# Two decoder layers on one core: q and k by features instead of by transposed tokens

## The chip, the cores and the metric

One core of a Trainium2 chip. The metric is the device time of one launch in microseconds. All arithmetic of the reference is in float32, and the kernel keeps nearly that precision in its big products by splitting each operand.

## The reference, cut

Two layers on 256 tokens of width 1024, with 8 heads of 128. Since the 256 keys are one block, layer 0's block-sparse attention is plain causal attention with a bias; layer 1 takes the difference of two softmax maps per head. Each layer ends in a SwiGLU of width 2816.

```python
for i in range(2):
    sh_a, sc_a, g_a, sh_f, sc_f, g_f = split(silu(c) @ ada_w[i] + ada_b[i])
    h = rms_norm(x, g0) * (1 + sc_a) + sh_a
    q, k, v = split(h @ w_qkv[i])                       # 256 x 1024 each
    # layer 0: p = softmax(q k' / sqrt(128) + bias), causal; o = p v
    # layer 1: heads in two halves of 64: a = softmax_1 - lam * softmax_2; o = rms_norm(a v)
    x = x + g_a * rms_norm(o @ w_o[i], g1)
    h = rms_norm(x, g2) * (1 + sc_f) + sh_f
    x = x + g_f * rms_norm((silu(h @ Wg) * (h @ Wu)) @ W_out, g3)
```

## The kernel before

**Tiles.** The 256 tokens are two tiles t = 0, 1 of 128. An activation that enters a big product lies transposed: `h[t]` is 128 features x (2, 8, 128): hi and lo part, 8 blocks k of features, 128 tokens. `h[t]` for t = 0 and t = 1 are buffers of two classes, `h0` and `h1`, one each.

**Products.** A float32 operand is split in hi (rounded to the fast type float32r) and lo (the rest). `mm` (line 488) makes a product of 128 tokens by up to 512 features for one block k in three passes q: hi x hi, hi x lo of the weights, lo of h x hi. For each pass and each output tile it issues one matrix instruction (line 492): the stationary operand is `h[t]` of that block, 128x128, and 512 columns of weights stream. In the profile each such instruction is a weight load (PEld) and a product (PE). Weights come by DMA into `raw` buffers (line 482), ScalarE writes the hi part (483), VectorE the lo part (484) into a ring of nine `s_...` tiles.

**q and k.** The scores need q and k with features on the partitions. `qk_T` (line 576) does it: ScalarE copies 128 tokens x 512 features out of PSUM (583; q is scaled there), PE transposes the four heads (`transposes`, 296), and ScalarE copies them into `qT` or `kT` (585), 128 features x 4 heads x 256 tokens. A group g is four heads.

**Order in layer 0.** `first_block` (675) makes q and k of group 0 and q of group 1 while the first modulation vectors are still loading: it goes through k in steps of 1, 2, 2, 2, 1 blocks, and for each step loads modulation weights, modulates both tiles' h (`modulate`, 500: ScalarE 508 and 513, VectorE 514) and adds the products of these blocks to six PSUM tiles. Then `build_bias` (316) makes the table of the relative bias in DRAM, from which `load_bias` reads it back by head; k of group 1, the scores and softmax of group 0 (`softmax`, 587: scores 603, bias 606, exp 611), v and the softmax of group 1 follow; `attend` (640) multiplies with v, and then come the output product, the norm and the feed-forward.

**Order in layer 1.** For each group and tile, q and k together (`mm` with two output tiles), then `qk_T` for both; v last.

**What sets the order of all work.** The functions only describe operations with engine, an assumed cost, and what they read and write. A planner (`Schedule`) issues them in the order that a table `PRIORITIES` of one number per operation and these costs lead to, under limits on buffers: PSUM tiles `a` (4) and `bc` (4), the classes `s2`, `raw`, `ring` and others. Each engine then works through its own queue in that order. All loads go through SP's queue.

Of the kernel before, what the change touches and what calls it, by code (L numbers as in the profile page):

```python
# [846 lines left out]
od6sF00000IRFg+0{{vD001xmMF124D*!<NSO9MTh5(!ZvjD^Z&j7mt+W_+c(*f!L^8rEuBLQmxc>#z4y#c)esR73UDFXcgv;md@*#YeV`T;Kjg#sG_Zvv+R  # L847
j{?>J9|AA|n*zZB0|Vv(F9T)+W&>^mQ~|#NCj;^TO#*`gjsvR$$OC%=p#!}G%mXI`mjvSj`2!FH!2^K=j0Cj<Uj%go8~}L$+yO%ZodLN3-U0>#E&>VybOWLT
cLIC@`2!*ZJp^h5R0K!_mIRUnodlc$0R%V%2n22gw*^rIxdr<L%>?iS3I(YJx&)^L;RGlJJ_S_;<OKu<8V0Kd`UDXLf(3#FF$PEmYXx@&eg=sK!UoL-Cj~PF
nFU-1X9jWx<N^r;N(6BPb^|Q~xCGw>zXMVO2L(9=n*-wmVFif=zy-<$)dl1QG6pRMH3lmMz6SdS2L@{gr3Xg_v<K@4fd-WZt_H;hLIzj{at4zI5eHNUYX_wV  # L850
=m!-D`UXA+f(I-Ja0rJ8*aq(gC<p%sSqNnalm?&%<OT`|LkLa?;slfgCI(9ez61vaYzCeNm<5Xk>;^^$xdq+@Z3mhMy9d$--3P`8BnT)7G6>)XMhJfhsRzXf
{0No@9SPwHhzNBEq6oPNu?X}C4hb{~y9m+<=?MP_d<pFdLkVRGlL@H_zzNq076~B<CJHeMbPCQ2EeSXYS_v8oJPJq(mj=8B{RcJ(Q3z`Y-v=oNMG0RCdI^*X
1PTudBnl`BGYSI;X$hzaJqlzBbqY`lp$g9me+rfgtP1c72MZ|++6v_gKnueP#S1(PDG4S3-Uw3)xC-V9c?(Mn=?wD<hYQ#X+Y0{+6by<Cv<v|aN(*ia!3$yw
NerS4ObD_GHwqpLQwv-Rs0*wMx(k&E`w4#v#0wq_cno+9lMI*)3<{A8E)1Rw)C?01Ee)s*v<*cGs|w-@zYWR_)(zne7!D*3ISyP7u@1Wo*bFiZpA6&-6%INM
$qrr)+z#&!X%E8?HxP9X4iJ<P%Mn%!kqgrc>I)VO7YrQ?hztV_PYqfPk`0{=Mh;O9cn*vXq7K*&<PPr+`VIyU5f3I0Uk|hoW)1fZ4-fYb91uYePY_!WsuA81
><!Eg@eWrHJ`Xz(%@A`C&Jykt4hy;r;tYZhnGdiJRSH`S2@S>%-4FB+pbLHtz6}ZxO%Ra~j19&Q0uYf9kr1d5UktDfOb)&f)e!6umI(_Bf(rr>84)27=?hN{
g$+g#T@iE<9S(mF$`6VW%@O1g{}CS&P7L%65e;SzGY_l}MG&bFoDk&@h!8gsZV_M+fDwlgC=*B%77aKJFAjeWtPa8s91rag1QHq&F%n1;ND|}{`w|foJ`+_F
YZHPKnG?nn=o2gyO%%x#Nf4P3;}LffUJ_Ci;1mrNDHcf<ixLYHVikrJo)y3q<`w!CVHSZF?Gf`8$`#QT0T*N#Z4t;49tn{O!wJp`Ee(_oN)0U!)D3VCQxCWh
R}1?P<PS;_P!Vntc?pdXjt;F7_!FTOIu@`IIub7xtQB?;CK4?Wj1q|v&k_g`DHFdCgcFn!78Irtbrf$C>J&;Ae-%|0iWPSjyB7Qv9u{pFB@>ktW)db9$`jrd
ToeHoyA+-lBNgoywG~zuZx+}WN*M<kG#SnqbQt>>e;7X*Um33%UJ{iOWfT7sHWXJBo(d}rD+~$`I1vF7<PS#?^AQRXXA{5^+!AFJu@nLnw-t64+7y`<92aaA  # L860
(iWZ<-4j9-P83-bWE5}|dlZHg>=gGDMirJ7+7;y$2NsPMCKt39$rs=k>=zCg85krOuM@iy0u>Dv85JZIQWaelXccr7xD~?{&lT|%KNd<Ck{6s8ychQuFc>=+
Mi^ZfIv8>oau}Hyrx<1!mKeww>KO1C5g8a6IvGeAX&I#%n;G31))~ba=Nb4J8yY+sJ{m0=0vhZZ0~;k9k`(q7fECdeH5bhn5*C6Mq!zChHy1(|SQlm&ZWntO
hZm?9)fWO7QW$6$tQfZ#!x-5Z<roqf9T_MYnHI(tiWrp`p&0NORT*I!Y#DbMgBgw)nHjqo#u?EW^BMjb2^tj|AQ~$gHyT13J{eaUWEp-Mj2e9zdm618&l=Sl
B^&)3P8(bsmmB39gB!RT9ULwkKO9gTXdH<g3mp0z*c<5^f*hwDQx<a<DHu%}WEy)Kx)z@p3mK6bs2aZ-Oc#n7z!}vV>>2|bc^6t4`574-FdIi3-xqWm@ETnk
bQ_Bs=N6+HN*kdY&Kvt19T;;Ps~Zs<C>%c=Y8gZu9UN60Y#f6eu^bT{&mYep&mWl_nH<L)-5m5B3mqXHI2}(NWgU|psU5%_*B$L01Rfh6UmkTHqaL{)=N|nY
D<4ZAYaiJk{~sS9jT<=~-yM7%F&;=BGaC*bP#%mP&>j>Y?i<n_7#<)Wd>?!tJQ{BurX7MGydMQ1W*DLy<QoMb4Ir5yUmV&V5g(c$o*?ZYgB_tB*dFa5iy@jJ
8y{96n;@DY%OSKP)FKQcfFrph{Ud51(jc87ogo(@7a|uT7a|uTP9jbsP9laPog(-mJR?#gX(KBnD<mr<cqES`>LfZPdL`o}114=I0~!e(Kpn3bJ0grCCmt9h
Pa_f`iX+4$&mTk}{2;_2#31Y;B_qQl+9S#$;UW$r@FNE#7bT`7yd={kh$Xfq%q1=*L?v4#Cmf$0xE?(qQy<PC+#L=fp&^JP79(mTiy_}6up|v8ofc0fIv0y3
!47jKsU|ru+AqB(%PlD`UoL|n03!e+G$czTVk8D0VIg5503~uIpCzOs3MD}$`6Uo0CMItlA|iGoJtkBpY9_WK0VFphm?khNT`1imJ|w0jbSRN1qbMaMjV8z@
xhTvi;wX|Mh9%S`_$VnUKPh1;eJPeI$tv_J#U|V)@+KfBHYa)~kte7pz9-cu>?av0Mkoy_St)BNk13let|`wc_9-ALHY!mn^eRXzIV?FWH7yGvlOo(AMkjG7  # L870
(I`<Ulqt_C=_C^;N++%+2`6MHfhJ8S0w~@o2P$hS)+!n+IV*oEu`0tVS1W5Psw?p-1S?1@yDQf#Dl7*iQYFqKm?eZI04Ja&gC}$(3n&UFO(=6FkSHo90x6j(
EiBnB6)ut}CMtR=j4MDabu5i1yeK~@g)E&cvn-e?#VhzL#w_0~^eogUbSk+j3oRinQZ30R#wiXeXf3QQ!z~pmPAi2g<t-5|5-wOOSS)`mKQ31;Yc3Ti`6)yy
fi9XZuP)IpyDwlcfiO)m$S&P3^)3uABQH@eW-om&lrO<A*)Q!c2rx7-NicOVxG=ad(J<&R{4f<UDltPbSuqqc-!uO+9yI?YxF_!?LoIMG`7cs0moOADP%9TN
*)ZlS6D(FNIW2xIku4oCjWC8WsxMeEZ!w%PJ2Fx-voXps;4x@2e=@8x4l<T98#Rb187jjnyetGO{4B*R2QCRIhAu`d#xBw;7%z<~e=jgFqA*J{VKas^4lgq>
&ox6g_cfh2O*is5i8o6*QaG(Sjyb<NQ8@xT{S`zzN)lo_qZ-#cAv_~JpgkZwcRXc2v_8czBQa_*_c0_g@G=`QK{9eO2QwZsG&6B9kulpbS2JxhgfloWb~39n
u`|ds^)t>c#W15W3p64$IW+Dvoix-m1T{!C=QVCG>@b8e6gDe1LN?_wRyB<^$~N~l+Bf?*YB)<djX91vPc&vUeKeCasx-hf*EH@lGBsZ{b~TJO&^1^#Z#ITD
oHnyI;5H;TJ2z4{Xg7a1oHyAw2RJ%7h&cW%D=tSbtuY=pRW>y>)HVw@i7)IoF*w6A+A^CnqcyrU{xuFa!#7GemN%?7@Hb&NcsQjv9XK>NjyMfDa5-=}zc|l0
<2W-t0zke#r9fjs+C%d~9YothAw@4kg+;GG!bNjK2u4drd`gW^tx#x0GDgKk1xR5=pGX}^1xw{fbxVdy@=GyJ^iWMoPEo&6|50mF|59sHtT0?Re>XrmKsmHI
wKA<W&o#?A);Z!iCNtqQ4K*7&EIKSY9x^;NT{U?-c{_SL7d3P_={bfwojbNWg*A{iu{OCoLOfYK**42K`#4-YX*_d0-8g7Ej5>2Xi9DS=x;)N2<UIR4DLrL5
d^v|Xk~y9^sX4$oIyyx<NIG#kaXOefm^zv|nmXY+DLW}UDLbM&ygL{?XFSI|-#pYk|2-x?m^M~8rZ}fJ&^bRkRxy?`<T6P*@jE{}?K$!}cRIZ~y*fHO{yRoI  # L880
t32C0`#k$R@;G=quREqV$vFo)Dm_#^Ts?<9hdrP@#y#Ra>^%uS7e4Ae2tGJIT0UStfj)>nsXn+q**^C^?LG}ZEI&Oz8$V7zW<QWWfIrYbkw2n8=s!$A*g70L
Z#&~V?>p)|!9C<X_dNwZ7(P2bPd-{cd_IUio<6ERlRmXRz&^}A*FNGt&pxw1^*-7^=sy8J*FP&j2|#5)gFuZytU$X!;Xn*Q^+0ApPeCj}K0#nXctM##l0l<E
#X+<|5JFi(^Eq2QmOP3-pg*}k5jv<l=sV9p=0E*E7dt0Cay=73DnLO%g*p&DIXzcEZa{=U&N_-b@I0G9vOvf{@;enidp_Sl_CO**d_6TlY(P0dP(ge_KR~-d
AVLO19Ydu<-$NHfIz+}p2Sg`CoI$cd$wA;j_CXCoBtkkuQ9@`!enOQ(tU|&<*+TF_G($>5VMBOBjzhvj%|q!!azv~}*F{o9xkT1P!Wk49F&U;A%R~o7UPYrt
c}0jtwnh9!ghazc<U|WaG)2!vzC{5>Kt^9i+(wB;=SF`<qegB<oJI{tPDj{0>poaNDnvp=UPLQADnfTcZAAV=7Da(PpFSTyDn&j;Sw-tWz(VXoW<`WWnMGnh
# [61 lines left out]
```

## Time and profile before

| | |
|---|---|
| time, median of 3 runs | 648.08 us (648.01 to 648.24) |
| the profiled execution, its own time | 645.48 us |
| its span, first to last instruction | 643.7 us |
| PE busy, VectorE busy, ScalarE busy | 627.5, 475.0, 372.5 us |
| loaded from DRAM | 158.69 MB |
| mean granted clock of PE | 0.999 |

A row of PE counts the time in which at least one product's record is open. The records overlap, so the sum of the groups is larger than this time, and the mean of a record is longer than the step from one product to the next.

### The profile page before, as it was taken

The numbers are of one execution on the slowest core, as the hardware profiler recorded it, in microseconds if no ns is written. First come the engines' busy times: TensorE is split into PE (matmuls) and PEld (weight loads), VectorE is DVE, ScalarE is ACT, GpSimd is POOL, SyncE is SP. The second block draws the span as 40 slices with busy tenths as digits, with TensorE's granted clock in tenths as the row PEclk, the third lists the DMA queues.
The fourth block names the chain that finished last, engine by engine and source line by source line (L and its number), as shares of the span: only waits on it lengthen the run. The fifth ranks groups of instructions, "written<-read, shape, count | busy, mean of one in ns | idle before, by whom it ended". The sixth has DMA issues, their size and how long they took to land.

```text
span 643.7 us, 8416 instructions
## 1 busy us (share of the span) xinstructions
PE 627.5 (97%) x2955; PEld 515.0 (80%) x2955; DVE 475.0 (74%) x602; ACT 372.5 (58%) x628; POOL 30.0 (5%) x66
## 2 busy tenths in 40 slices
...
GB/s 291 360 363 319 300 378 381 347 292 249 301 285 353 363 313 270 233 174 293 351 233 194 291 218 271 133 229 72 190 262 163 187 272 224 250 199 180 128 1 66
DMA packets 72487, 160.58 MB, mean 249 GB/s; under 512 B 5491, under 2 KB 22516, under 8 KB 72444
## 3 DMA queue, kind: packets, MB, share of 16 engines
...
q14 instruction: 20, 0.16, 0.1%
q10 hardware_dynamic: 192, 0.08, 0.0%
HBM read 158.69 MB, written 1.33 MB: 249 GB/s over the span
## 4 chain that ended last, share of the span: by engine, by line
PE 85%; DMA 5%; DVE 3%; ACT 3%; POOL 2%; issue 1%; SPq 1%; DVEq 0%; POOLq 0%; ACTq 0%
PE pf L492 19%; PE pg L492 16%; PE pu L492 16%; PE pq L492 10%; PE pv L492 6%; PE po L492 5%; PE pgu L492 3%; DMA bias<-toep 3%; PE ps L603 2%; PE pa L296 1%; PE po L649 1%; PE ph L296 1%; ACT hm L508 1%; DMA toep<-bd 1%; PE pg L419 1%
## 5 line engine op out<-in xcount | busy, mean ns | idle before, releaser
L492 PE MATMUL pg<-s_i,h 128*128 128x512 f32 x480 | 188.3, 392 | 0.0
L492 PE MATMUL pu<-s_i,h 128*128 128x512 f32 x480 | 187.1, 390 | 0.0
L484 DVE TENSOR_TENSOR s_i<-w_i,s_i 128x1024 fp32r<-128x1024 f32 (+1 forms) x96 | 107.0, 1133 | 50.7 <-ACT s_i L483 49.7
L492 PE MATMUL pf<-s_u,a 128*128 128x512 f32 x528 | 137.4, 392 | 0.0
L483 ACT ACTIVATE s_i<-w_i 128x1024 fp32r<-128x1024 f32 (+1 forms) x96 | 93.1, 989 | 73.3 <-PE pu L492 48.8
L492 PEld LDWEIGHTS pf<-s_u,a 128*128 128x128 f32 x528 | 97.9, 188 | 20.4 <-ACT s_u L483 0.4
L492 PEld LDWEIGHTS pg<-s_i,h 128*128 128x128 f32 x480 | 90.1, 188 | 18.8 <-DVE s_i L484 0.3
L492 PEld LDWEIGHTS pu<-s_i,h 128*128 128x128 f32 x480 | 90.1, 188 | 18.4
L362 DVE SCALAR_TENSOR_TENSOR acc<-aw,cact,acc 128x1024 f32<-128x1024 f32 x70 | 89.3, 1277 | 2.2 <-DMA aw<-in_ada_w_dram 1.8
L483 ACT ACTIVATE s_u<-w_u 128x1024 fp32r<-128x1024 f32 x44 | 46.4, 1059 | 58.3 <-PE pu L492 28.8
L484 DVE TENSOR_TENSOR s_u<-w_u,s_u 128x1024 fp32r<-128x1024 f32 x44 | 53.6, 1221 | 30.2 <-ACT s_u L483 29.8
L492 PE MATMUL po<-s_o,o 128*128 128x512 f32 x192 | 49.8, 399 | 0.0
L492 PE MATMUL pq<-s_q,h 128*128 128x512 f32 x192 | 47.7, 397 | 1.8 <-ACT h L513 1.8
L492 PEld LDWEIGHTS pq<-s_q,h 128*128 128x128 f32 x192 | 35.0, 188 | 10.5 <-ACT h L513 2.5
L484 DVE TENSOR_TENSOR s_q<-w_q,s_q 128x1024 fp32r<-128x1024 f32 x32 | 38.5, 1220 | 5.9 <-ACT s_q L483 5.6
L492 PEld LDWEIGHTS po<-s_o,o 128*128 128x128 f32 x192 | 34.9, 188 | 6.8 <-DVE o L665 0.4
L492 PE MATMUL pq<-s_q,hq 128*128 128x512 f32 x144 | 37.0, 408 | 2.5 <-ACT hq L513 2.5
L483 ACT ACTIVATE s_q<-w_q 128x1024 fp32r<-128x1024 f32 x32 | 33.3, 1054 | 4.8 <-PE pq L492 2.0
L492 PEld LDWEIGHTS pq<-s_q,hq 128*128 128x128 f32 x144 | 27.5, 195 | 9.2 <-ACT hq L513 3.0
L471 POOL TENSOR_SCALAR ms<-ss 128x1 f32<-128x1 f32 x16 | 7.3, 459 | 504.7 <-ACT z L542 497.9
L611 ACT ACTIVATE sx<-sx,mx 128x128 f32<-128x128 f32 (+1 forms) x48 | 21.3, 445 | 10.6 <-DVE mx L609 10.6
L492 PE MATMUL pgu<-s_i,h 128*128 128x512 f32 x96 | 26.1, 392 | 0.0
...
## 6 DMA issues: line engine op xcount, KB each, us to landing
...
```

The lines of the kernel that those rows point to most:

```text
L296: nc.tensor.transpose(dst[:, o:o + n], a, ident[:n, :n])
L362: op("DVE", tt(n) + 0.065, lambda: nc.vector.scalar_tensor_tensor(a.t, w(), cact[:, kc:kc + 1], a.t, op0=OP.mult, op1=OP.add), r=[cact, w. ...
L419: nc.tensor.matmul(pg[:, n * j + b:n * j + b + 1], w[:, e, j, b * 128:b * 128 + 128], cact[:, kc + e:kc + e + 1], start=kc + e + j + b == ...
L471: op("POOL", 0.16, lambda: nc.gpsimd.tensor_scalar(ms.t, m0.t[:], 1.0 / n, EPS, op0=OP.mult, op1=OP.add), r=[m0], w=[ms])
L483: op("ACT", ac(2 * n), lambda: nc.scalar.activation(b[:, 0], w.t[:], AF.Copy), r=[w], w=[(b, K(0))], name="hi" + name)
L484: op("DVE", tt(2 * n), lambda: nc.vector.tensor_sub(b[:, 1], w.t[:], b[:, 0].bitcast(F)), r=[w, (b, K(0))], w=[(b, K(1))], name="lo" + name)
L492: nc.tensor.matmul(p[:, :n], a, b[:, 1 if q == 1 else 0, s], start=first and q == 0, stop=last and q == 2)
L508: op("ACT", ac(128, 2, fps), lambda i=i, k=k: nc.scalar.activation(m[:, i], src[2](i), AF.Identity, bias=sh[:, k:k + 1], scale=G[:, k:k + 1]),
L603: nc.tensor.matmul(p[:, i * nk:i * nk + nk], qT[rows, h0 + i, t * 128:t * 128 + 128], kT[rows, h0 + i, 0:nk], start=True, stop=True)
L611: op("ACT", ac(nk, 2), lambda i=i, sx=sx, mx=mx, su=su: nc.scalar.activation(sx[:, i], sx[:, i], AF.Exp, bias=mx[:, i:i + 1], accum_out=su ...
L649: nc.tensor.matmul(p[:, i * 128:i * 128 + 128], a, b, start=kt == 0, stop=kt == t)
```

## The change

A new function `mmT` makes the same three passes with the roles exchanged: 128 columns of the split weights are stationary, and the 256 tokens of both tiles stream. The output is 128 features x 256 tokens, two heads to a PSUM tile, so q and k come out as the scores need them, and `qk_F` copies them with one ScalarE instruction. For one instruction to stream both tiles' h, all `h` buffers become the two halves of one tile `hh`. Layer 0 uses this for q and k of both groups, layer 1 for the second group. What the scores depend on is stated by pairs of heads where it was stated by token tiles. In layer 0 the softmax of tile 0 of group 0 is described ahead of k of group 1. The table of priorities is another one.

```diff
+    hh = const.tile([128, T, 2, KC, 128], R, name="hh")
+    def mmT(ps, h, k, W, first, last):
+        def f(q):
+            for p, (b, s, c) in zip(ps, W):
+                for j in range(2):
+                    nc.tensor.matmul(p[:, j * 256:j * 256 + 256].rearrange("p (t q) -> p t q", t=T),
+                                     b[:, 1 if q == 1 else 0, s, c + j * 128:c + j * 128 + 128], hh[:, :, 1 if q == 2 else 0, k],
+                                     start=first and q + j == 0, stop=last and q == 2, skip_group_check=True)
+        for q in range(3):
+            op("PE", 2 * len(ps) * 0.12, lambda q=q: f(q), r=[(h[t], K(10 + k if q == 2 else k)) for t in range(T)] +
+               [(b, K(1 if q == 1 else 0)) for b, _, _ in W], w=list(ps), main=True, name="mm" + W[0][0].name)
...
+    def qk_F(st, l, g, w, ps, hp):
+        if g not in st[w]:
+            st[w][g] = Buf(f"{w}{g}", f"{w}{g}", [128, 4, 256])
+        dst = st[w][g]
+        sc = (128 if l == 0 else 64) ** -0.5 if w == "qT" else 1.0
+        op("ACT", ac(512, 0, True), lambda: nc.scalar.activation(
+            dst[:, 2 * hp:2 * hp + 2], ps.t[:].rearrange("p (h q) -> p h q", h=2), AF.Copy, scale=sc), r=[ps], w=[(dst, K(hp, 2 + hp))])
...
-                op("PE", 0.88 if l == 0 else 0.54 if t else 0.95, f, r=[(qT, K(t)), (kT, KR(0, t + 1))], w=[p], main=True, name="S")
+                op("PE", 0.88 if l == 0 else 0.54 if t else 0.95, f, r=[(qT, hk[t]), (kT, hk[0] | hk[t])], w=[p], main=True, name="S")
...
-        ps = [[Buf("pq0", "a"), Buf("pq1", "a"), Buf("pq2", "bc")] for t in range(T)]
+        ps = [[Buf(f"pq{i}{p}", "a" if i < 2 else "bc") for p in range(2)] for i in range(3)]
...
-            for t in range(T):
-                for k in ks:
-                    mm(ps[t][:2], h[t], k, W[k - k0], 512, k == 0, k == KC - 1)
-            for t in range(T):
-                for k in ks:
-                    mm(ps[t][2:], h[t], k, [W2[k]], 512, k == 0, k == KC - 1)
+            for k in ks:
+                mmT(ps[0] + ps[1], h, k, [(W[k - k0][s][0], s, c) for s in range(2) for c in (0, 256)], k == 0, k == KC - 1)
+            for k in ks:
+                mmT(ps[2], h, k, [(*W2[k], c) for c in (0, 256)], k == 0, k == KC - 1)
...
-            for t in range(T):
-                qk_T(st, l, t, 1, "qT", ps[t][2])
-                qk_T(st, l, t, 0, "qT", ps[t][0])
-                qk_T(st, l, t, 0, "kT", ps[t][1])
-            W = []
-            for t in range(T):
-                p = Buf("pk1", "a")
-                for k in range(KC):
-                    if t == 0 and k % 2 == 0:
-                        W.extend(qk1(0, k, D + 512, 2))
-                    mm([p], hT[t], k, [W[k]], 512, k == 0, k == KC - 1)
-                qk_T(st, l, t, 1, "kT", p)
-                softmax(st, l, t, 0)
+            for i, w, g in ((0, "qT", 0), (1, "kT", 0), (2, "qT", 1)):
+                for p in range(2):
+                    qk_F(st, l, g, w, ps[i][p], p)
+            W, ps = [], [Buf("pk1", "a") for _ in range(2)]
+            softmax(st, l, 0, 0)
+            for k in range(KC):
+                if k % 2 == 0:
+                    W.extend(qk1(0, k, D + 512, 2))
+                mmT(ps, hT, k, [(*W[k], c) for c in (0, 256)], k == 0, k == KC - 1)
+            for p in range(2):
+                qk_F(st, l, 1, "kT", ps[p], p)
+            softmax(st, l, 1, 0)
...
-                        mm(ps, hT[t], k, W[k], 512, k == 0, k == KC - 1)
-                    qk_T(st, l, t, g, "qT", ps[0])
-                    qk_T(st, l, t, g, "kT", ps[1])
+                        if g == 0:
+                            mm(ps, hT[t], k, W[k], 512, k == 0, k == KC - 1)
+                        else:
+                            mmT(ps, hT, k, [(*w, t * 256) for w in W[k]], k == 0, k == KC - 1)
+                    for w, p in zip(("qT", "kT"), ps):
+                        if g == 0:
+                            qk_T(st, l, t, g, w, p)
+                        else:
+                            qk_F(st, l, g, w, p, t)
...
+            if b.cls in ("h0", "h1"):
+                b.t = hh[:, int(b.cls[1])]
+            elif b.cls and b.t is None:
```

## Rows read from the trace of the kernel before

**Rows 1.** The page: busy us, share of the span and instructions by engine.

```profile
PE   627.5 (97%) x2955; PEld 515.0 (80%) x2955; DVE 475.0 (74%) x602; ACT 372.5 (58%) x628; POOL 30.0 (5%) x66
```

**Rows 2.** The chain that ended last: start, us until the next piece, what.

```profile
100.53 0.87 PE ps L603 x4
...
110.51 1.78 PE po L649 x16
...
355.76 0.87 PE pqk L296 x8
...
627.25 6.35 PE pf L492 x28
```

**Rows 3.** Groups of PE and of its weight loads, by shape.

```profile
L492 PE MATMUL pq<-s_q,h 128*128 128x512 f32 x192 | 47.7, 397 | 1.8 <-ACT h L513 1.8
L492 PE MATMUL pq<-s_q,hq 128*128 128x512 f32 x144 | 37.0, 408 | 2.5 <-ACT hq L513 2.5
...
L492 PE MATMUL pk<-s_q,hq 128*128 128x512 f32 x48 | 14.5, 411 | 0.0
...
L296 PE MATMUL pqk<-ident,qk 128*128 128x128 f32 x64 | 9.3, 275 | 0.5 <-ACT qk L583 0.5
...
L492 PEld LDWEIGHTS pk<-s_q,hq 128*128 128x128 f32 x48 | 8.7, 188 | 1.5
...
L649 PEld LDWEIGHTS po<-PT,v 128*128 128x128 f32 x48 | 6.0, 191 | 0.3
```

**Rows 4.** Busy time of each engine by stretch: stretch, its length, engines, clock, DMA.

```profile
core 0: us, PE busy (x) PEld busy (x) DVE busy (x) ACT busy (x) POOL busy (x), PEclk, DMA share, GB/s
...
21.20:56.00 34.80, 34.00 (x154) 27.36 (x154) 31.43 (x57) 22.77 (x38) 0.00 (x0) 1.00 1.08 369
56.00:80.00 24.00, 24.00 (x124) 20.10 (x124) 15.78 (x17) 17.69 (x25) 0.00 (x0) 1.00 0.91 282
80.00:112.00 32.00, 31.05 (x163) 25.53 (x163) 30.43 (x38) 25.83 (x65) 0.00 (x0) 1.00 0.99 381
...
329.00:346.00 17.00, 14.79 (x71) 11.66 (x71) 10.49 (x15) 13.22 (x30) 3.02 (x5) 1.00 0.60 211
```

**Rows 5.** The first copy of the transposed evacuation: ns min/median/max, first and last start.

```profile
L583 ACT ACTIVATE qk<-pq x14: 576/598/637, 58.0 to 392.7; 128x512 f32<-128x512 f32 x14
```

**Rows 6.** Instructions in order of time, 20 to 30 us: start, us, what, idle before.

```profile
20.81 0.49 ACT L513 ACTIVATE hq<-hm 128x128 fp32r<-128x128 f32 x2
...
21.16 4.47 PE L492 MATMUL pq<-s_q,hq 128*128 128x512 f32 x12 [1.68 <-ACT hq L513]
...
28.24 0.40 ACT L513 ACTIVATE hq<-hm 128x256 fp32r<-128x256 f32 x1
...
28.69 1.66 PE L492 MATMUL pq<-s_q,hq 128*128 128x512 f32 x6 [0.80 <-ACT hq L513]
29.06 0.42 ACT L513 ACTIVATE hq<-hm 128x256 fp32r<-128x256 f32 x1
```

**Rows 7.** Waits of PE: waited for, us in total, times, longest.

```profile
PE pq L492 <- ACT hq L513: 2.5, 2, 1.7
...
PE pqk L296 <- ACT qk L583: 0.5, 1, 0.5
PE ps L603 <- ACT kT L585: 0.4, 2, 0.2
```

**Rows 8.** The chain that ended last, 57 to 87 us.

```profile
57.61 7.57 DMA toep<-bd
...
68.32 8.22 DMA bias<-toep
...
76.56 9.68 DMA bias<-toep
```

More of the change, by code (lines that the diff above doesn't have):

```diff
@@ L596, in softmax @@
             P, rr = [], []
+            hk = [frozenset(2 * i + h // 2 for h in range(h0, h0 + nh)) for i in range(T)]
             for m in range(1 + l):
@@ L851 @@
[L851 to L855, printed above, removed]
@@ L911 @@
-7kMIiad~}th<THFdwHpOsd>+N-g%#S&3XTMAbKi#OL_
+F993?000008~_LaApipa1pq4mKmalTNdR8}b^wh4qX4=9(E#EA?ErQHC;|BZivlPC`2ZsUkO4OVxB=e*6aq>D00JHYvjS8Ct^siY*8%nc1p+7nfdV`Ntpdve
+;{t>M&;r2#{Q?RBDg(g*R|BU5qXVu33IcEg(*v9W5d=*HxC8D33<S#q=mS3l3IsX?lLTr6vINQm<^WUxlmfc~XaRWu;sOc-odBT$G6PxzO9AEqf&;Px-2><Y
+{sZ#^76cjuNd!^@zXbLK2n22g#|3o++XXKMW&~3NpajnZdIXIGuLR%(5(QcXiUqm_76x7h;sp8xLIo`bjs~U%cLGxa@&g_OEd%5Nh6Jtz2?OH;E(KNvn*+ZC
+eg&ol00#913kK>1BnBV`D+Xf))CLL%1qM+E#Rs7V2M9h0Zw6Zii3Z~aH3moqm<F*1_6A1>cL%2j8wgDZz6RC?0|<TylnAW|Q3S^X3I=foC<R9anFh-Spalj6
@@ new lines @@
+HV0k@#04}4g$JYu*9W8r?FZrq76=ju90=+LTL_T|qX!8IK?!RJ(FqF*NeG_^#0c~Vj0iUfvk1-z+z1T`f(fw+@CiZ+Jqc6^Z3!w0ZwiVESO$Ftz6bsXAP9E|
+pa(Mt;s^!_A_+|i9tz<JL<&d>QVK)|MG1uoTMB^+unKJoj0(L9p9<3o1Pe6_JPU9O`vd?0=>;YSn+p62YzsRJfeTIx;tQJ#s|?2sjtq4T+6%T0@(xuGHxL&O
+Di4|v(h#N)wGhM*_z+MLDhP=Q(+PbGiwmj?!V3lrN({3I846YkVhnl=k_@U0?hFPEtO_a&$P6A0HVsY<W(}(i!wp6W!wL%v@(ni*d=8WjtPaEuJrCv%9t`mf
+77mgQIu1+^un)u!!x0)1!VIJi)D8*{bPt*jRuF0s%Mj}jY6^u6kPLnelnvVr)d{l;>I(`EAP!FsN(+b#0S#sj+z#^&{0Ni^%?dUTOb`DL#0}UFC=hTEhY++7
+at;U(VG!XE4iO{~9}4;lF$_BqXc2!A7z|?#xDA#OtPx=nkrJsApAO^<RS&!l(+{2y+7K2IJrOAp0}-(i=n_E_!4hf{hZCn0j}N8~ybl%-ED%EwS`eNPQW4n^
@@ new lines @@
+@DT<Q9TGGWN)mVyjuNF3=@S1E785NKLlasPzY|&$V-L{}ybyp9Xc4RtcoPQ_+7$d03J>@YQW4J*4ij(_>l4=#9u+<n4G265MhTA!TotbsuMsU1j|uh)vkN*6
+X$yP}g$)o701Z<QMhuk?un+1HAPwpf{0r(4Ru1YB*bYz=bQ7r)&l4vTu@fZ}-4qQEau8+_@e&>pG!thM?Gu#}FBESR`xML(RTYmEwG}uPsTMOA;}^LWdKi2c
+3>dx`Iuwu<t`tZX=M;+;K^4swCKC`Bn-x+Q;T5bGxfV$n1{o0<0U7HU;25?TAsO`;HyK$Oyb|{klN0R|E)+Kvix4srfD%Fw*AYh&4Gw`1?+<bhs1Xhl`43_e
+xDo;q{}XEz-4aF=q!hRlVHFP+ofE(l%M)G{brc5`G!?rQ#ufh+Ll#aJSr%m$a2ALbh!&C-ofaV%KNnsXX%~tYaT9zK))V3r8WcPfNEA~PY83Dk{1i$R%oW`g
+=oR!83Kq^54Hpd;4i^s>4;K^{pci--#~0NX<QM1{ju$5w1{hBmZ5VeLmKdcN+88kz#uz~vbQxnAg&CF^t{Ko77#ar}*%`<gFdAkWfE45ukriPT#TD@tKNVIL
@@ new lines @@
+78W5EEEX6SN*7TVcNd@+wim${5EwETK^R6DSr}g!a2S9XiWr|5y%@(B5*4%-mlv!T&KKMl^B4LTAQ&eYnHbO*Ss7#*Zy9?Th8d9=of)VZvl+h`${E!e>lo`9
+5g8F0AR0RvCK^N<gc_+D#~RTZ@EZOaGaF$W9~(;>jvJpFup7Y}*&F&B^Ba8|1RQG{92`9yF%|_F?HJ)1_Zbcva2D1Vg%~9oI~r0NN*B8rT^VT_e;Sq=lNSdW
+mKm)Y!y4Ke0T+xI?iukK2OAz6+!uKo-WoL<cN>lyrWi^Zr5dFhyBpFQB^VVOfE(!>{~Hz@HyoB6{T?bGfgdd#LmXNhaU9$n+#K8-+#K8-{2UY=B^@{&W*vMT
+n;o_t+a2Q_3LY*VK^|xxbRN7O?H*wtc^{Y`tr?FT#T-=~&mAcqAsYZ4L>-GBv>v}6t{H_J!yCyS-yR(wH5#5B>>Vs0KOd<diW^WJb{*g!@E@}vI31TB3LnKF
+*dX&D3LRP=nI0h_Vj&zN!yEP;F&;`H<s$bYA0wh8-y{DcIwcDrD<C`|P#|X@e;}D43L!TkP9b_Blp(1h?jZysHX>glaUzT&qawT_%pw&dDkDrIg(Ea5hA5>d
@@ new lines @@
+NEzlDM;jCwq#)ZMI38ah5+RBoCn9Phbsvf!%^#c}!y(!s4J7X*1tmWtT_f`&9VIg*NhKg8IV4jg|0NYBEGB9sjU}WdfF0i+!5ujt>>0NoB_B5+gC2e$93f02
+4I{oJ|09(p9TeIo0TjF@@DKziRVdOZ{3sqLZYpCd;wyz9gd)!(b0dQzn<K^`*dh=ku_MkSf+SBL^&u=GktD4oy(Fm~IU#W&)+AshcO|MKCM8`ZyCu;j=p|Jl
+V<QbDLnc`!ohFSWO(ugT%O)i!JSX@cvLWgrQYU~XttZYW?I#{6J}7f2a3+T)v?ll_X(y&9#3%752q;P@VJLVgjwq!l04WzKL@8S-aVdx?pDD~K<0<(m9xBBu
+O)G6H#4AuFnI#P-dM2JIQz>64?<qDaF(y_h!zke<4=36uyeKUxwJGT+Cn`NE5GqtEfhub%uPVhV+$yLmzAFhUH!FH887xLDp)7DBkt5I{&Lb-#KqOWpi6o07
+0VUTX(Iv|yMkb#n1t)qZ8Yx*Y>oCJ6zbXAGm@4xsAS)9k)h0nFkt@|J>?>3!J}Q+e3oJM+W-OH{v?}T<iY(4704-M~<|iB|7cD3)Pc5A%At{R~b1jH1nJo+_
```

101 lines of the change are left out of this document (40 added, 61 removed).

## The prediction

> **What bounds the kernel now.** I read the page first: the matrix engine (PE) is busy in 627.5 of 643.7 us, VectorE in 475.0, ScalarE in 372.5 [rows 1]. A busy PE row is a count of overlapping records, so I went on to the chain of waits, in which a run of products shows its true step. In the stream of the second feed-forward 28 products of 512 columns take 6.35 us, 226.8 ns each [rows 2]; their records are near 400 ns long [rows 3] because each one overlaps the next. So PE is paced by the number of its instructions and columns, and each instruction that goes away is worth its step and not its record. Then I read the busy time by stretches [rows 4]: in the four stretches that hold the changed work of layer 0 and the start of layer 1, PE is without work for 0.80, 0.00, 0.95 and 2.21 us. Time saved on PE is therefore time saved at the end, unless something else is just behind it. In layer 0 something is: from 80 to 112 us VectorE is busy in 30.43 of 32 us, and the DMA share is 0.91 to 1.08 from 21 to 112 us [rows 4].
>
> **What goes.** Twelve of the sixteen transposed evacuations go: eight in layer 0, four in layer 1 (q and k of the second group of heads). Each is a ScalarE copy of 598 ns in the median [rows 5], four transposes and a second copy; one copy stays. ScalarE loses 12 copies, 7.2 us, but it isn't the bound (25.83 of 32 us at its busiest here [rows 4]), so I count nothing for that. PE loses 48 of the 64 transposes [rows 3]. Eight of them take 0.87 us in the chain [rows 2], 109 ns each: 48 x 0.109 = **5.2 us** off PE, 3.5 in layer 0 and 1.7 in layer 1.
>
> **What is added.** The same products are made with the weights as the stationary operand and 256 token columns streaming, where before a token tile was stationary and 512 weight columns streamed. 144 + 48 products of layer 0 and half of the 192 of layer 1 [rows 3], 288 in all, become 576 of half the width, each with a weight load of its own. Before they cost 288 x 0.2268 = 65.3 us. No row shows a product of this type at 256 columns, so its step is bounded from rows near it.
>
> Below: the products of probabilities with v have the same 128x128 load, of 191 ns as against 188 [rows 3], and 16 of them take 1.78 us, 111 ns each [rows 2]. Their 128 columns go at half the speed: four score products of 256 columns of that type take 0.87 us, 217 ns each, almost as long as 512 of the streamed type. So 111 ns is what loads and streams of the new size have been seen to do side by side, though each load's own record is longer: 576 x 0.111 = 63.9 us, 1.4 less than now. Half of the present step, 113.4 ns, gives 65.3, nothing more than now. Above: taken at one cycle a column, 512 columns at 2.4 GHz (granted clock 1.00 [rows 4]) are 213.3 ns, so the present step has 13.5 ns beside its columns. If these belong to the instruction, the new step is 106.7 + 13.5 = 120.2 ns, and 576 cost 69.2 us, 3.9 more. A step of 113.4 if the surplus goes with the columns, 120.2 if with the instruction: the rows at one width can't say which. The slow score products have 3.7 ns beside the same 213.3, which tells nothing of this type. Both ends are near; I take the middle, 116.8 ns: 67.3 us, **2.0 us more**.
>
> The Trainium skill says in Perfetto Trace Analysis, section Optimizing Tensor Performance, that larger matmuls are more efficient than smaller ones where they are possible. That speaks against this change, and by it the upper step would hold (3.9 more), by the bare halves of the present row none (0 more).
>
> **The first block waits for both token tiles.** One new instruction streams both tiles' h. Now PE starts at 21.16 us, as soon as ScalarE has the first tile's h; the second's takes half of 0.49 us more: +0.24. At 28.69 us it starts again on the first tile's h, which ends at 28.64, while the second's ends at 29.06 + 0.42 = 29.48 [rows 6]: +0.84. These are the only two waits of its products for this h, 2.5 us in all [rows 7]; later PE has a backlog, and the second tile's h is early enough. Sum **+1.1 us**, behind which PE's whole queue stands.
>
> **Waits that go.** In layer 0 PE waits 0.5 us for a copy that feeds a transpose and 0.4 us for the copy behind one [rows 7]. The chain product, copy, transpose, copy, scores becomes product, copy, scores: **-0.9 us**. What is late next there is the bias: table written from 57.61 us for 7.57, read in two waits that end at 86.24 [rows 8]. The scores may now be made earlier, but VectorE's addition of the bias can't, and what is queued behind it on VectorE, such as the splitting of v's weights, would wait with it.
>
> No DMA is added or moved to another queue by the edits; the order of all work is that of a new table, so loads may be issued in another order on SP's queue. I cost that at nothing. The first product group of layer 1 keeps its old form, so the idle time around the arrival of its h (2.21 us in 329 to 346 [rows 4]) stays as before. The shared tile for h takes the place of two tiles of the same total size, so no buffer is lost; buffers for the intermediate copies and their transposes in PSUM are freed, at no counted gain.
>
> **Sum.** -5.2 + 2.0 + 1.1 - 0.9 = **-3.0 us**. The profiled execution took 645.48 us (span 643.7 and 1.8 around it), so it would take 642.5. The median of the runs is 2.6 above that execution, and the same difference from it gives 648.08 - 3.0 = **645.1 us**. With steps of 113.4 and 120.2 ns it is 643.1 and 647.0.
>
> **Rivals.**
> - *Layer 0 keeps its length.* VectorE, the loads and the bias set the end of attention there, and PE only waits elsewhere for what it has saved. For it: VectorE at 95% and the DMA share near 1 [rows 4], and the chain that runs through the bias from 57 to 86 us [rows 8]. Against it: PE itself has next to no idle time there, and VectorE is busy in only 15.78 of the 24 us before 80 us, so that work can move forward. Then only layer 1 gains: -1.7 + 192 x 0.0034 = -1.1, **647.0 us**.
> - *Slower: load and stream share one supply.* The present step serves 512 columns streamed and 128 loaded in 226.8 ns. If that is one rate for both, 256 + 128 columns take 136 ns, 576 of them 78.3 us, 13.0 more than now: -5.2 + 13.0 + 0.2 = +8.0, **656.1 us**. The change loses from a step of 122 ns on ((65.3 + 5.0) / 576), and measurably so, by 1.3 us, from 124.3. For it: this type streams a column in half the time of the type in which 111 ns was seen, so it asks for its operands twice as fast. Against it: the load's record is 188 ns beside these products and 191 beside the slow ones [rows 3].
> - *Every group of the first block waits.* If all five groups, not two, wait for the second tile at 0.84 us each, three more make +2.5: -0.5, **647.6 us**. Against it: no wait is shown after the second.
> - *The new order also closes idle time.* PE's idle time in the four stretches is 4.0 us [rows 4]; if three quarters of it went as well, it would be -6.0, **642.1 us**. Nothing in the profile speaks for or against it.
>
> **Chances.** Forecast 0.45, layer 0 keeps its length 0.20, shared supply 0.12, waits in every group 0.10, better order 0.13. A difference of 0.2%, 1.3 us, is about what a measurement of this kernel can tell from no change: below 646.8 is faster, above 649.4 slower. The forecast is faster but for its upper edge (0.43 of 0.45), the better order all of it, a third of the first rival (0.06): 0.62. Slower are the shared supply and a fifth of the waiting groups, where they also delay the weights: 0.14. The rest, 0.24, is the same. The range runs from 642.0 (the better order, and the lower step) to 649.0 (the waiting groups with the upper step, 649.5, nearly): it leaves out the shared supply and the edges of two others, under 2 in 10.
>
> **What would show it.** Transposes of q and k: 16 in place of 64. Runs of 256-column products in the chain of waits: their step near 117 ns, between 113 and 120; above 122 the forecast is wrong in sign. PE's first wait for h about 0.24 us longer, the second 0.8, and no third. In layer 0 no wait of scores for a transposed k. If the end of layer 0's attention (the first product with the output weights, 106 us now) has not moved by about 2 us while the step is right, layer 0 is bound elsewhere. What would make it wrong: a step outside these bounds, new idle time of PE between 56 and 112 us, or an order that loses elsewhere, which would show as idle time of PE in the feed-forward stretches.

## The result and the profile after

The kernel became slower: 653.67 us in the median of five runs (650.97 to 655.56) against 648.01 (646.84 to 648.24) of the kernel before, a ratio of 1.0084 [1.0059, 1.0109], or +5.4 us [3.8, 7.1]. The forecast was 645.1, the range 642.0 to 649.0. The profiled execution took 653.67 us, its span 651.6, 7.9 more than the span before.

Of the page after, the busy times, which answer to [rows 1]:

```profile
PE 635.5 (98%) x3195; PEld 527.5 (81%) x3195; DVE 474.4 (73%) x602; ACT 368.0 (56%) x616; POOL 30.6 (5%) x66
```

PE is still busy nearly all the time, and for 8.0 us more, although transposes went. The groups by shape, which answer to [rows 3], say that the change is there: 576 products of 256 columns, and 16 transposes of q and k where there were 64.

```profile
L506 PE MATMUL pq<-hh,s_q 128*128 128x256 f32 x480 | 62.7, 288 | 0.0
...
L506 PE MATMUL pk<-hh,s_q 128*128 128x256 f32 x96 | 13.1, 286 | 0.0
...
L296 PE MATMUL pqk<-ident,qk 128*128 128x128 f32 x16 | 2.4, 272 | 0.0
```

The chain that ended last, which answers to [rows 2] (start, us until the next piece, what), gives the steps. After:

```profile
96.92 3.74 PE pv L492 x16
...
370.67 2.35 PE pq L506 x20
...
431.69 7.00 PE po L492 x30
...
539.57 3.66 PE pf L492 x16
```

Before, from the same chain:

```profile
96.00 3.64 PE pv L492 x16
...
442.77 5.91 PE po L492 x26
```

The new products step 2.35 / 20 = 117.5 ns: inside the bounds of the prediction and next to its 116.8. What is new stands in the other lines. Products that the change doesn't touch, the same 512 columns from the same weights, take 233.8 ns (`pv`) and 233.3 (`po`), where they took 227.5 and 227.3 before. Those of `pf`, 228.8 in this piece, are nearer to the 226.8 of before [rows 2]; over all steps of `pf` the mean is 231.3, against 227.7 before. `pv` and `po` have h's tile as their stationary operand (attention's output lies in it too), `pf` has not.

PE's waits, which answer to [rows 7], and the busy time by stretches, which answers to [rows 4] (from 24 us, since PE's first product of q starts at 24.21 now):

```profile
PE ps L628 <- ACT kT L609: 3.0, 1, 3.0
```

```profile
24.00:56.00 32.00, 32.00 (x251) 31.16 (x252) 29.03 (x51) 20.17 (x33) 0.00 (x0) 1.00 1.04 344
56.00:80.00 24.00, 24.00 (x186) 23.19 (x185) 16.80 (x21) 15.36 (x23) 0.00 (x0) 1.00 0.94 300
80.00:112.00 32.00, 29.00 (x139) 23.62 (x139) 27.50 (x38) 26.68 (x68) 0.00 (x0) 0.95 0.98 348
335.00:352.00 17.00, 16.51 (x75) 12.85 (x74) 15.79 (x20) 14.15 (x30) 4.15 (x6) 1.00 0.94 326
```

From 80 to 112 us PE is without work for 3.00 us, 2.05 more than before, and its granted clock is 0.95 there. At the start of layer 1 it is without work for 0.49 us instead of 2.21. So the new order loses in one place and gains in another. In order of time, 80 to 92 us:

```profile
82.53 1.29 DVE L631 TENSOR_TENSOR sx<-ps,bias 128x512 f32<-128x512 f32 x2 [3.47 <-DMA bias<-toep]
...
84.44 0.51 ACT L636 ACTIVATE sx<-sx,mx 128x256 f32<-128x256 f32 x1 [3.10 <-DVE mx L634]
...
85.82 0.58 ACT L609 ACTIVATE kT<-pk 128x512 f32<-128x512 f32 x1
...
86.45 2.08 PE L628 MATMUL ps<-kT,qT 128*128 128x256 f32 x4 [3.00 <-ACT kT L609]
...
87.96 2.52 PE L492 MATMUL pv<-s_q0v,hh 128*128 128x512 f32 x6
```

VectorE waits 3.47 us for a bias load; three exponentials on ScalarE wait for VectorE; the second copy of k stands behind them in ScalarE's queue, though its product had ended at 80.7; the scores wait for that copy. Right behind this wait six products take 2.52 us, and the granted clock of the two stretches of 4 us there is 0.78 and 0.80 (below): a part of them ran at the lower level, 1.2 GHz.

Last, the front. In order of time:

```profile
5.83 0.35 SPq L277 DMA_DIRECT2D c<-in_c_dram  x1
...
14.36 6.96 PE L419 MATMUL pg<-cact,aw 128*128 128x1 f32 x32 [0.17 <-ACT xT L709]
...
22.52 1.84 PE L374 MATMUL pg<-ones,a 128*128 128x1 f32 x8 [1.20 <-DVE a L362]
...
24.21 1.20 PE L506 MATMUL pq<-hh,s_q 128*128 128x256 f32 x4
```

The first product starts at 24.21 us, 3.05 later than in [rows 6], and not because of the second token tile: c is loaded later, and eight products of the modulation now stand right ahead of it. How much of the 3.05 us is the order isn't shown: in d1 below, with the same front, the same 32 products of the modulation take 4.36 us instead of the 6.96 here, and the first product starts at 20.57. Neither of the two waits for h that the prediction priced is there.

Two theories follow. **Addresses**: h in one tile lies elsewhere in SBUF, and the products that read it step more slowly for that. **Order**: the new table costs the time, by the wait near 86 us and the later front.

### The profile page after: what moved, and what is told of

Read it like the earlier page. It is cut to its first block, busy times and chain, and to the rows that moved or that the text cites. A ratio compares the mean times of both kernels' runs of the same rounds, so it can differ in the third digit from the quotient of the medians.

```text
span 651.6 us, 8859 instructions
## 1 busy us (share of the span) xinstructions
PE 635.5 (98%) x3195; PEld 527.5 (81%) x3195; DVE 474.4 (73%) x602; ACT 368.0 (56%) x616; POOL 30.6 (5%) x66
## 4 chain that ended last, share of the span: by engine, by line
PE 83%; ACT 5%; DMA 4%; DVE 4%; issue 2%; POOL 1%; DVEq 0%; ACTq 0%; POOLq 0%; SPq 0%
PE pf L492 18%; PE pg L492 17%; PE pu L492 17%; PE pv L492 6%; PE po L492 6%; PE pq L506 5%; PE pgu L492 3%; PE ps L628 2%; PE pq L492 2%; PE po L674 2%; DMA bias<-toep 2%; PE pa L296 1%; DVE a L362 1%; DVE s_q L484 1%; PE pg L419 1%
## 5 line engine op out<-in xcount | busy, mean ns | idle before, releaser
L492 PE MATMUL pg<-s_i,hh 128*128 128x512 f32 x480 | 190.5, 397 | 0.0
L492 PE MATMUL pu<-s_i,hh 128*128 128x512 f32 x480 | 189.6, 395 | 0.0
L492 PEld LDWEIGHTS pu<-s_i,hh 128*128 128x128 f32 x480 | 90.2, 188 | 21.5
L492 PEld LDWEIGHTS pg<-s_i,hh 128*128 128x128 f32 x480 | 90.1, 188 | 21.5 <-ACT s_i L483 0.2
L506 PE MATMUL pq<-hh,s_q 128*128 128x256 f32 x480 | 62.7, 288 | 0.0
L506 PEld LDWEIGHTS pq<-hh,s_q 128*128 128x128 f32 x480 | 60.2, 194 | 2.4 <-issue 1.0
L492 PE MATMUL po<-s_o,hh 128*128 128x512 f32 x192 | 51.0, 405 | 0.0
L492 PEld LDWEIGHTS po<-s_o,hh 128*128 128x128 f32 x192 | 34.6, 189 | 7.4 <-ACT hh L688 0.4
L636 ACT ACTIVATE sx<-sx,mx 128x256 f32<-128x256 f32 (+1 forms) x48 | 21.3, 445 | 11.4 <-DVE mx L634 11.2
L492 PE MATMUL pgu<-s_i,hh 128*128 128x512 f32 x96 | 26.8, 397 | 0.0
```

Of the source, the lines that this page charges most:

```text
L492: nc.tensor.matmul(p[:, :n], a, b[:, 1 if q == 1 else 0, s], start=first and q == 0, stop=last and q == 2)
L506: nc.tensor.matmul(p[:, j * 256:j * 256 + 256].rearrange("p (t q) -> p t q", t=T), b[:, 1 if q == 1 else 0, s, c + j * 128:c + j * 128 + 1 ...
L636: op("ACT", ac(nk, 2), lambda i=i, sx=sx, mx=mx, su=su: nc.scalar.activation(sx[:, i], sx[:, i], AF.Exp, bias=mx[:, i:i + 1], accum_out=su ...
```

## Experiments on the addresses

From the built programs: each tile's address is that in one partition, in bytes. Before, h's two tiles lay at 122304 and 130496, the streamed weights in a ring of nine buffers; all of these addresses leave 64 when divided by 128. In the changed kernel `hh` is a constant tile at 26976, which leaves 96; the ring still leaves 64. Five kernels place h differently and leave every instruction's work and order as it is (some small constants move with it); two shift all buffers of the kernel before.

**Changed kernel, h at 16512** (a1). The order of the constant tiles is changed, so that h comes first; the ring stays where it was.

```diff
+    hh = const.tile([128, T, 2, KC, 128], R, name="hh")
     xt = [keep(f"x{t}", [128, D]) for t in range(T)]
...
-    hh = const.tile([128, T, 2, KC, 128], R, name="hh")
```

> The changed kernel with the shared tile hh as the first constant, so that it begins at a multiple of 64 bytes in each partition (16512) and not 32 bytes behind one (26976); same instructions, same order. Theory (a stationary operand that begins 32 bytes off a 64-byte multiple slows every product of 512 columns): these step in 227 to 228 ns in the mean again and not 233, 2060 x 5.3 = 10.9 us less less what one buffer of a, still 32 off, keeps: 642 to 644.5 us, 0.6 to 0.9% faster than before. Rival (the new order makes other engines' traffic slow the products): 233 ns and 653 us as in the changed kernel. Rival (one tile among the constants, wherever it lies): 653 us too.

Measured: 649.22 us, ratio 1.0027 [1.0015, 1.0039], 0.57% less than the changed kernel. Theory and rivals miss: the step falls to 229.9 ns, not to 227 to 228, and the time to neither 642 to 644.5 nor 653. A multiple of 64 is not the condition.

**Changed kernel, h at 16544** (a2). 32 bytes further, with `cact` ahead of `hh`.

```diff
+    cact = keep("cact", [128, KC])
+    hh = const.tile([128, T, 2, KC, 128], R, name="hh")
+    ones1 = keep("ones1", [128, 1])
     xt = [keep(f"x{t}", [128, D]) for t in range(T)]
...
```

> As a1_hh_first, but hh begins 32 bytes behind a multiple of 64 (16544), with the constants around it changed in order only. Theory (offset): 233 ns a product and 651 to 655 us, as the changed kernel, although hh lies 10 KB from where it lay there. Rival (the place in memory, not the offset): as a1_hh_first.

Measured: 654.12 us, ratio 1.0091 [1.0058, 1.0123]. 32 bytes take back all that a1 gained, so it isn't the neighbourhood in SBUF but the remainder.

**Kernel before, its two h tiles in one at 16512** (b1), **and at 16544** (b2), there with `cact` ahead of it as in a2.

```diff
+    hh = const.tile([128, T, 2, KC, 128], R, name="hh")
...
-            if b.cls and b.t is None:
+            if b.cls in ("h0", "h1"):
+                b.t = hh[:, int(b.cls[1])]
+            elif b.cls and b.t is None:
```

> The kernel before, its products and order untouched, but all h buffers are halves of one tile hh, first of the constants, at a multiple of 64. Theory (offset): no change, 647 to 649 us, 227 to 228 ns a product. Rival (one shared tile): slower, toward 657 us.

> As b1_before_hh, with hh 32 bytes behind a multiple of 64. Theory (offset): all 1776 products of 512 columns whose stationary operand is h or the attention's output step about 233 ns, 1776 x 6 = 10.7 us more: 657 to 660 us. Rival (the new order, or anything of the exchanged roles): no change, 648 us.

Measured: 651.52 us, ratio 1.0066 [1.0046, 1.0087], and 655.71, ratio 1.0136 [1.0115, 1.0158]. The kernel before, with its own order and its own products, loses as much and more from an address alone. b1's theory, no change at a multiple of 64, misses like a1's; b2's has the step (233.2 ns) and nearly the cost: 10.7 us expected, 8.8 measured.

**Changed kernel, h at 16576** (d1), where the remainder is the ring's. As a2, with `ones1` ahead of `hh` too.

```diff
     cact = keep("cact", [128, KC])
+    ones1 = keep("ones1", [128, 1])
     hh = const.tile([128, T, 2, KC, 128], R, name="hh")
-    ones1 = keep("ones1", [128, 1])
```

> The changed kernel with hh at 16576, which is 64 over a multiple of 128 bytes, as all tiles of split weights are; same instructions and order. The runs so far: difference of stationary and streaming address modulo 128 of 0: 227 to 228 ns a product; 64: 229.8; 32 or 96: 233.3. Theory (this difference sets the step): 227.7 ns in the mean again, 1770 x 2.2 = 3.9 us less than a1_hh_first, and products of 256 columns near 113 ns in place of 113 to 118: 643 to 645.5 us, faster than before by the 3 to 4 us that the other steps of the prediction gave. Rival (h as one tile among the constants slows by itself, as the first two runs that were aligned to 64 left open): as a1_hh_first, 649 us.

Measured: 646.00 us, ratio 0.9988 [0.9972, 1.0005]. The 512-column step is back at 228.0 ns, as the theory had it. The products of 256 columns, expected near 113 ns, step 119.5, and the time stays above the theory's 643 to 645.5; it can't be told from that of the kernel before.

**Kernel before, all buffers 32 bytes lower** (d4), **and at multiples of 128** (d3). Does each address count, or the difference of the two operands?

```diff
-    ones1 = keep("ones1", [128, 1])
-    mh = keep("mh", [128, 4])
+    small = const.tile([128, 8], F, name="small")
+    const.tile([128, 8], F, name="pad")                 # d3 only
+    ones1 = Buf("ones1", t=small[:, 0:1])
+    mh = Buf("mh", t=small[:, 4:8])
...
-        e, nl, sg = keep("le", [128, 2]), keep("nlam", [128, 1]), keep("sg", [128, 128])
+        e, nl, sg = Buf("le", t=small[:, 1:3]), Buf("nlam", t=small[:, 3:4]), keep("sg", [128, 128])   # d3 only
```

> The kernel before with two small constants merged, so that every buffer behind them, weights, h and a alike, lies 32 bytes lower: all stationary and streaming tiles begin 32 over a multiple of 128, and their differences stay 0. Theory (the difference counts): no change, 647 to 648.5 us, 227 to 228 ns. Rival (each operand must begin at a multiple of 64): all 2378 products of 512 columns slow, 233 ns or more, 658 us or more.

> As d4_before_shift32, but 64 bytes lower: both operands begin at multiples of 128. Theory (the difference counts alone): no change, 647 to 648.5 us. Rival (the 13.3 ns beside the columns come from operands 64 off a multiple of 128): steps below 226.7 ns, down to 216, and up to 25 us less.

Measured: ratios 1.0005 [0.9992, 1.0018] and 0.9997 [0.9985, 1.0009]. No change: with both operands shifted alike, none of the three remainders (64, 32, 0) is better than another.

All steps together. A step here is the time between the starts of two such products that follow each other, behind 32 us, worked out from the records, with gaps that hold something else left out (250 ns and more for 512 columns, 170 for 256); "512" takes the products that read h.

```
kernel            h minus ring,   mean step ns   256 columns    ratio
                  modulo 128      512 columns    mean, median
before                  0             227.7          -          1
before, d4, d3          0          227.8, 227.8      -          1.0005, 0.9997
changed, d1             0             228.0       119.5, 120    0.9988
before, b1             64             229.7          -          1.0066
changed, a1            64             229.9       115.4, 114    1.0027
before, b2             96             233.2          -          1.0136
changed, a2            96             233.1       118.3, 117    1.0091
changed                32             233.4       118.1, 118    1.0084
```

The same thing in pieces of the chain: sixteen `pv`, thirty `po` and sixteen `pf` products, first of d1 and then of a1:

```profile
93.94 3.66 PE pv L493 x16
...
425.20 6.84 PE po L493 x30
...
531.56 3.65 PE pf L493 x16
```

```profile
96.22 3.69 PE pv L493 x16
...
428.79 6.90 PE po L493 x30
...
535.83 3.65 PE pf L493 x16
```

`po` goes from 7.00 us (changed kernel) over 6.90 to 6.84 as the difference goes from 32 over 64 to 0; this piece of `pf`, which doesn't read h, stays at 3.65 (the mean of all its steps is 230.5 ns in a1 and 229.6 in d1). And b2, the kernel before with a difference of 96:

```profile
99.89 3.74 PE pv L493 x16
...
592.88 3.63 PE pf L493 x16
```

What follows: the step depends on where the stationary and the streamed operand lie with respect to each other, modulo 128 bytes. With 1536 products that read h, 5.7 ns each are 8.8 us against the kernel before. Against d1 it is 5.4 ns each, 8.3 us, less 0.8 for the 576 products of 256 columns, which step 1.4 ns more in d1. The spans of the changed kernel and of d1 differ by 651.6 - 642.0 = 9.6 us, of which 3.6 lie ahead of the first product; the ratios differ by 0.96%, 6.2 us. In the kernel before 1824 products read h: 5.5 ns each are 10.0 us, measured +8.8 [7.5, 10.2]. Why the chip does so is not shown.

## Experiments on the order

**d1 with one copy moved** (f1). The second copy of k stands behind the first one in ScalarE's queue, ahead of the three exponentials.

```diff
             o.prio = float(p) / 50
+        self.ops[332].prio = 76.3                       # was 78.02
```

> The changed kernel with h's tile at address 16576 (d1_hh_same_residue, 646.0 us) and one instruction moved on ScalarE: the second copy of the keys of the second pair of groups (kT from pk) stands right behind the first one instead of behind three exponentials that wait for a late bias load. Theory (the order's wait is a second cost, apart from the addresses): the copy runs near 79 us instead of 82.85, TensorE's wait of 2.3 us at 83.5 us goes, and with it the stretch at half clock right behind it (six 512-column products in 2.95 us instead of 1.4), so 3 to 4 us come off: 642 to 643 us. Rival 1 (the late bias sets the end of the attention of layer 0 in any order): the wait moves to the next instruction that needs the bias's results, 645.5 to 646.5. Rival 2 (the half clock has nothing to do with the wait): 2.3 us come off and a half-clock stretch stays, about 643.7.

Measured: 646.05 us, ratio 0.9966 [0.9949, 0.9984], against d1's 0.9988: 1.4 us, but the two intervals overlap. The wait for the copy is gone, and two others stand behind it. The longer of these waits of PE, and the chain, of f1:

```profile
PE pv L493 <- DVE s_q0v L485: 1.5, 1, 1.5
```

```profile
72.17 10.65 DMA bias<-toep
...
82.90 1.29 DVE sx L631 x2
...
84.82 2.36 ACT sx L636 x10
87.17 0.95 ACT s_o L484
88.12 0.80 ACT sx L645 x2
88.92 1.91 ACT s_q0v L484 x2
...
90.86 1.23 DVE s_q0v L485
...
92.13 2.38 PE pv L493 x6
```

The late bias still holds ScalarE up; now the conversions of v's weights stand behind it, and PE waits 1.5 and 0.7 us for those. PE is idle for 2.17 us from 80 to 112, where it was 2.33 in d1. The 3 to 4 us of the theory did not come; rival 1 had the mechanism, the wait that moves on, and its time, no gain, is not excluded.

**The changed kernel with the same copy moved by the same line** (f3), h still at 26976.

> The changed kernel as it is, h's tile at its own address 26976, with only the copy of keys moved ahead of the three exponentials. Theory (two separate costs that add): the addresses' cost of about 8 to 10 us stays, the wait of 3.0 us and the half-clock stretch of 3.4 us behind it go, so 653.7 less 3 to 5 us: 649 to 651 us, and the mean step of 512-column products stays near 233 ns. Rival (the late bias sets the end in any order): 653 to 654.

Measured: 652.62 us, ratio 1.0081 [1.0068, 1.0094], against 1.0084: no difference that can be told, nearer to the rival. The step stays at 233.4 ns, and the addresses' cost with it.

**f1 with c loaded early** (f2).

```diff
+        for i, p in ((332, 76.3), (0, 0.7), (21, 6.0), (24, 9.0), (80, 9.2), (50, 11.7), (52, 12.65)): self.ops[i].prio = p
```

> As f1_copy_ahead, and the front put nearer to the order of the kernel before: the load of c stands third in SyncE's queue instead of ninth, its transpose stands ahead of those of x, and ScalarE takes its activation ahead of the copies of x. Theory (the front's order costs too): the first product of the layer starts 1 to 1.4 us earlier than in f1_copy_ahead, 0.5 to 1.5 us faster than it. Rival (the front ends with the loads of the modulation weights, whatever c does): as f1_copy_ahead within 0.5 us.

Measured: 644.49 us, ratio 0.9962 [0.9947, 0.9977], f1 within 0.04%: the rival. In this execution the first product starts at 20.45 us, against 24.02 in f1's; but d1, without the early c, had 20.57, so that isn't shown to be c's doing.

**f2 with three bias loads early** (f4).

```diff
-... (52, 12.65)): self.ops[i].prio = p
+... (52, 12.65), (281, 65.5), (404, 66.1), (407, 66.2)): self.ops[i].prio = p
```

> As f2_copy_ahead_early_c, and on SyncE three bias loads stand ahead of four weight loads: the last part of the first bias tile and two parts of the second. In f2 VectorE waited 2.4 and 3.4 us for these loads at 76 and 81 us, ScalarE's exponentials and behind them two conversions of value weights stood behind that, and TensorE waited 0.9 and 1.5 us for those conversions near 88 to 91 us, with a stretch of half clock after it. Theory (the late bias is the root of the order's cost in the attention of layer 0): both waits go and no half clock follows, 2 to 4 us faster than f2: 641 to 643 us. Rival (the loads that are pushed back by the bias loads, the value weights among them, are late in its place): TensorE waits as long for the same conversions, now for their loads, and the time is that of f2, 644 to 645.

Measured: 642.71 us, ratio 0.9942 [0.9922, 0.9961], 0.20% or 1.3 us less than f2, and the intervals overlap. The theory had 2 to 4. The time itself lies in its range, but the kernel before took 646.63 us beside f4 and 647.47 beside f2. Busy time of f4 from 80 to 112 us, and its chain:

```profile
80.00:112.00 32.00, 30.50 (x162) 25.56 (x161) 29.09 (x37) 26.60 (x62) 0.00 (x0) 1.00 1.01 371
```

```profile
75.40 9.91 DMA w_o<-in_moba_w_o_dram
...
85.33 1.06 ACT s_o L484
86.39 1.90 ACT s_q0v L484 x2
...
88.35 1.23 DVE s_q0v L485
...
89.62 1.67 PE pv L493 x6
```

PE's idle time is 1.50 us instead of 2.33 in d1 and 3.00 in the changed kernel. The bias is off the chain; a load of output weights has taken its place, and of f2's two waits the one of 1.5 us is left.

**f4 with the value weights ahead of the output weights** (f5).

```diff
-... (407, 66.2)): self.ops[i].prio = p
+... (407, 66.2), (384, 70.6), (568, 74.0), (569, 82.2), (570, 84.0)): self.ops[i].prio = p
```

> As f4_bias_early, with one load of value weights ahead of one of output weights on SyncE, and its conversions on ScalarE and VectorE ahead of those of the output weights. In f4 the copy of the output weights on ScalarE began at 85.33 us, when its load had landed (9.9 us in the chain), and the two conversions of value weights stood behind it; TensorE waited 1.5 us for them at 88 to 89.6 us. Theory (what is left of the wait is the order of loads on one queue and of copies on ScalarE): the wait goes, 1 to 2 us faster than f4: 641 to 642 us. Rival (the output weights, now later, are waited for at the first output product near 106 us, or the value weights' load ends no sooner): as f4 within 0.5 us, about 642.7.

Measured: 644.04 us, ratio 0.9934 [0.9913, 0.9954], f4 within 0.08%: the rival. The wait for `s_q0v` falls to 0.6 us, and PE waits 1.2 us for ScalarE's normalized probabilities instead.

f4 and f5 beat both kernels: by 0.58% [0.39, 0.78] and 0.66% [0.46, 0.87] the kernel before, by about 1.4% the changed one. Two thirds of the second figure, 0.96%, are the place of h.

## Why the prediction was wrong

**The step that failed** is the sentence on the shared tile: it "takes the place of two tiles of the same total size, so no buffer is lost". No buffer was lost, but the tile's address changed, and with it the step of 1536 products that the change does not otherwise touch, from 227.7 to 233.4 ns: 8.8 us by the steps, 6.2 by the ratios of the changed kernel and d1, where the sum had nothing. Without it, in d1, the change gives 0.9988 [0.9972, 1.0005], -0.8 us [-1.8, +0.3], which can't be told from no change; with it, +5.4. No row of the trace of before could have priced it, since there every product that reads h had the difference 0; but the prediction could have said that the tile moves.

**Transposes**, -5.2: 16 are left of 64, as stated.

**The step at 256 columns**, taken at 116.8 between 113.4 and 120.2: 118.1 in the changed kernel, 119.5 in d1, 115.4 in a1. So the bounds held. Which of the two is right depends on the addresses. At the kernel before's own difference, 0, it is the upper one: beside the columns as the prediction counts them (106.7 and 213.3 ns) 12.8 ns are left at 256 and 14.7 at 512, so the surplus goes with the instruction. At 64 (a1) 8.7 and 16.6 are left, and it goes with the columns. At 0 the 576 products cost 68.8 us, +3.5 instead of +2.0, and the prediction's sum becomes -1.5 us, which lies in d1's interval. That is partly luck: of the terms below, the +1.1 in it did not come, and what the order did is not in it. Larger matmuls are more efficient than smaller ones, the Trainium skill says (Perfetto Trace Analysis, Optimizing Tensor Performance); d1's 119.5 against half of 228.0, 114.0, agrees; a1's 115.4 against 115.0 hardly shows it. The shared supply (136 ns) is excluded by all of these steps.

**The first block's wait**, +1.1: not there. The first product comes 3.05 us later, but not for h. The front differs between executions too: in d1 the first product started at 20.57 us, in f1, with the same front, at 24.02. So what the order of the front costs stays open.

**Waits that go**, -0.9: the wait for a copy that feeds a transpose went, but the scores wait for the copy of k for 3.0 us instead of 0.4. The prediction had named what comes next, the bias. But it put the wait on VectorE's queue, where v's weights would stand behind it; it was ScalarE's queue, where first the copy of k and, with that moved, v's weights stood. What the prediction named as making it wrong, "new idle time of PE between 56 and 112 us", is there.

**The order**, costed at nothing: it lost and gained. In d1 PE's idle time from 80 to 112 us grew by 1.4 us (29.67 of 32 busy) and the clock of 0.95 took another 1.6; at the start of layer 1 1.5 us of idle time went (0.69 left of 2.21):

```profile
80.00:112.00 32.00, 29.67 (x146) 24.68 (x145) 30.23 (x40) 27.94 (x67) 0.00 (x0) 0.95 0.94 345
329.00:346.00 17.00, 16.31 (x75) 12.89 (x75) 15.78 (x20) 14.14 (x29) 3.95 (x6) 1.00 0.93 327
```

The prediction had said that the second of these stays as before, since that product group keeps its form; the order moved it all the same. That is +1.5 us in sum, in this one execution. The feed-forward of layer 0 starts at 139.68 us in d1 and at 139.84 in the kernel before, the first products at 20.57 and 21.16. In these two executions layer 0's attention kept its length without the addresses' cost, as the first rival had it (647.0, or 0.9983; d1 has 0.9988). With priorities moved, f5 came to 0.9934, seven tenths of the way to the rival of the better order (642.1, or 0.9908).

Open is the rest of the sum. The terms named here for the changed kernel (-5.2, +2.7 for 118.1 ns, +8.8, the wait and its clock +3.7, the idle time of layer 1 -1.7) make +8.3, where spans differ by 7.9 and medians by 5.4; the front (+3.05 at the first product) is in none of them, nor are the 528 products `pf`, whose mean step is 231.3 ns in the changed kernel and 229.6 in d1 against 227.7. These don't read h, but one of their four stationary buffers has a difference of 32 in both kernels. With the records matched in order to the built programs, in d1 the products with that buffer step 232.6 ns and the others 228.1, so the difference explains d1's mean; in the changed kernel the others step 230.6, and why is not shown.
